# The last product of a decoder layer: twelve pairs of tiles in seven products, with their weight sums made by GpSimd and kept in DRAM

## The chip, the cores and the metric

One program on 1 core of a Trainium2 chip. The metric is device microseconds for one execution; the kernel before took 1563.09 us, the median of three runs (1562.99, 1563.09, 1564.04). Lower is better.

## The reference

One layer of a decoder on 256 tokens of width 2048, in float32. Three token mixers (a convolution A, a spatial gate B, a sparse attention C) are merged channel by channel by sigmoid gates, then a gated feed-forward of width 5632 follows. Cut to what matters here:

```python
h = rms_norm(x, w_pre);  p = h @ w_in                 # A, B, C inputs and 3 x 2048 gate logits
y = (g_A * A + g_B * B + g_C * C) @ w_o;  x = x + rms_norm(y, w_post)
h = rms_norm(x, w_pre2); u = causal_dwconv3(h @ w_up)
x = x + rms_norm((silu(u_g) * u_v) @ w_down, w_post2) # w_down: 5632 x 2048, "the last product"
```

## The kernel before

**Products.** Every float32 product is made as three TensorE products of rounded numbers: a weight tile arrives by a DMA of SyncE's queue in a buffer `wraw` (five of 128x1024, 512 KB each), ScalarE copies it, rounded, to `whi` (four), VectorE writes the remainder `wraw - whi` to `wlo` (four), and TensorE multiplies hi by hi, hi by lo and lo by hi. A load can be issued only when its buffer's last reader is done.

**Stages.** They follow each other on TensorE: the input projections (to about 296 us); the gating projections, function `branch`, with products `pg` and `py` (296 to 757); the product with `w_o` (757 to 842); the up projection (860 to 1325.7); the last product (1325.7 to 1553.4). In `branch` the work of the three mixers is cut in steps by Python generators, and `pump(BUDGET)` puts steps between the gating products. One of these steps is the compression of the attention's keys and values: `cmp_prep` copies pieces of `kd` into tiles `bt` (VectorE), whose last column GpSimd zeroes (`G.memset(tmp[:, :, :, 15], 0.0)`, L613), and splits them into `bk`, which TensorE takes in `zp`.

**What sets the order.** Up to the gating a scheduler with priorities orders the instructions of each engine. The splits of the weights follow a fixed order from `w_o` on, and in the last product everything does: `fixed` chains each instruction of ScalarE and VectorE behind the one before it, and `in_line` does so for TensorE. GpSimd has 48 instructions: some loads at the start, the copies to `kd`, the memsets of `bt`, the loads of `x2`, and `kept_y` and `yb`, by which the feed-forward's residual goes to DRAM and comes back.

**The last product.** The 44 tiles of 128 rows of `w_down` are taken in two halves of 1024 output columns (`Pair(0)`, `Pair(1)`). A plain tile costs 4 blocks x 3 = 12 matmuls of 128x512. Two tiles together are also done as a Strassen-like 2x2 product (Winograd's form): seven products instead of eight, 21 matmuls instead of 24. For that `quad` loads two pieces `b` and `a` (four blocks of 128x512) and forms four sums of them on VectorE, between the splits:

```python
fixed(V, V.tensor_sub, tt[:, L], b[:, L], a[:, U])
fixed(V, V.tensor_sub, a[:, U], a[:, U], a[:, L])
fixed(V, V.tensor_sub, tt[:, U], b[:, L], a[:, U])
fixed(V, V.tensor_sub, b[:, U], b[:, U], tt[:, U])
```

The sums of the activations of a pair are made by `sums` during the up projection. `EARLY` names ten such pairs, `PLAIN` the other 24 tiles; the last six of these are kept (`KEEP`), split in advance, and used block by block at the end of the second half: first tokens 0 to 127 with output columns `n` = 0 and 1, then tokens 128 to 255. Behind each block VectorE adds the side products (`result`), ScalarE squares, and after each token half come the norm (L247 to L250), the weighing by the gain, the scalings with the residual `yb` (L1418) and the writes. Tile `fin`, in the place that `hT` had, holds the results, the gain and two scratch pieces for the sums.

Of the kernel before, what the change touches and what calls it, by code (L numbers as in the profile page):

```python
# [31 lines left out]
T = 256  # L32
# [22 lines left out]
def block(ctx: ExitStack, tc: tile.TileContext, x, xf, fp, cst, rows, sgw, w1, w2, wf_a, wt_bv, wf_bu, wf_c,  # L55
# [289 lines left out]
    rh = PZ.tile([128, 2], F32, name="rh")  # L347
# [530 lines left out]
    BUDGET = BG  # L878
    mac = s16(P0, [128, 2, D], F32, "mac")
    mix = {}  # L880

    def branch(bi, act_of):

        for cb in range(4):
            pg = [PS.tile([128, 512], F32, tag="acc", name=f"pg{bi}{cb}{t}") for t in range(2)]
            for q in range(4):
                hs = granule(wt_g[(bi * 4 + cb) * 4 + q])
                for k in range(4 * q, 4 * q + 4):
                    hi, lo = hs[(k % 4) // 2]
# [15 lines left out]
            for q in range(2):  # L905
                hs = granule(wt_p[(bi * 4 + cb) * 2 + q])
                if cb == 0 and q == 0:
                    until("BAC"[bi])
                    if bi == 2:
                        mix["h"] = s16(P1, [128, KT, T], R, "mh")  # L910
                        mix["l"] = s16(P1, [128, KT, T], R, "ml")
                act = act_of()
                for k in range(4 * q, 4 * q + 4):
                    hi, lo = hs[(k % 4) // 2]
                    c = slice((k % 2) * 512, (k % 2) * 512 + 512)
                    for t in range(2):
# [105 lines left out]
    for cb in range(3):  # L1022
# [21 lines left out]
    for n, (cb, p) in enumerate(HELD):  # L1044
        for i in range(2):
# [184 lines left out]

    P2c = ctx.enter_context(tc.tile_pool(name="p2c", bufs=1))
    fin = P0.tile([128, 7168], F32, tag="hT", name="fin")
    res = fin[:, 0:4096].rearrange("p (t n) -> p t n", t=2)
    gain = fin[:, 4096:5120]
    turn = [0]

    def scratch():
        turn[0] ^= 1  # L1240
# [9 lines left out]
    def high(hi, x):  # L1250
        fixed(S, S.activation, hi, x, AF.Copy)

    def rest(lo, x, hi):
        fixed(V, V.tensor_sub, lo, x, hi.bitcast(F32))

    def weights(src, into=None):
        raw = fetch(src, 1024)
        hi, lo = (into[:, 0], into[:, 1]) if into is not None else ring(raw.name)
        high(hi, raw)
        rest(lo, raw, hi)  # L1260
        return hi, lo

    def ring(name):
        return P0.tile([128, 1024], R, tag="whi", bufs=4, name=f"whi{name}"), rests(f"wlo{name}")[:, 0:1024]

    class Pair:
        def __init__(self, p):
# [25 lines left out]

        def quad(self, j):

            k0, k1 = EARLY[j]
            last = j == len(EARLY) - 1
            b, a = (fetch(wt_dq[self.p, j][:, x:x + 1024], 1024) for x in (0, 1024))
            L, U = slice(0, 512), slice(512, 1024)
            nm = f"q{self.p}_{j}"  # L1300
            tt = scratch()
            (hb, lb), (ha, la), (ht, lt) = (ring(nm + x) for x in "bat")
            h4, l4 = (P2c.tile([128, 512], R, tag=tag, name=f"{tag}{nm}") for tag in ("h4", "l4"))
            high(hb, b)
# [12 lines left out]
            s1, s2, s4 = ((sh[:, i], sl[:, i]) for i in range(3))
            for bank_, act, (h, l), c in (
                    (self.c[0][1], s4, (hb, lb), L), (self.c[0][0], g2(k1, H1), (hb, lb), U),
                    (self.p1, g2(k0, H1), (ha, la), L), (self.p5, s1, (ha, la), U),  # L1320
                    (self.p7, g2(k0, H2), (ht, lt), L), (self.p6, s2, (ht, lt), U),
                    (self.c[1][0], g2(k1, H2), (h4, l4), L)):
# [37 lines left out]
    first, second = Pair(0), None  # L1360
    i = 0
    for j in range(NQ):
        while i < 3 + (NP - 6) * j // (NQ - 1):
            first.plain(i)
            i += 1
        first.quad(j)
    for i in range(i, NP):
        first.plain(i)
    first.combine()
    second = Pair(1)  # L1370
    kept = []
    i = 0
    for j in range(NQ):
        while i < 3 + (NP - KEEP - 3) * j // (NQ - 1):
            second.plain(i)
            if i == 2:
                for t in range(2):
                    for n in range(2):
                        first.result(t, n, fixed)
            elif 3 <= i < 7:  # L1380
                first.weigh((i - 3) // 2, (i - 3) % 2, fixed)
            elif i == 9:
                nc.sync.dma_start(gain, row(3072, 1024))
            i += 1
        second.quad(j)
        if j == len(EARLY) - 1:
# [3 lines left out]
        for x in range(0 if j < NQ - 5 else 1 if j < NQ - 1 else KEEP - 4):  # L1390
            k = NP - KEEP + len(kept)
            into = None
            if j < NQ - 1:
                kt = P2.tile([128, 11, T], R, tag=("gh", "gl")[j % 2], bufs=4, name=f"kept{k}")
                into = kt[:, 0:8].rearrange("p (a b) c -> p a (b c)", a=2)
            kept.append((PLAIN[k], weights(wt_dn[1, k], into)))
    assert i == NP - KEEP and len(kept) == KEEP
    second.combine()
    for t in range(2):
        for n in range(2):  # L1400
            c = slice(n * 512, n * 512 + 512)
# [20 lines left out]
def _layout(inp):  # L1422
# [110 lines left out]
```

## Time and profile before

| | |
|---|---|
| median of the runs | 1563.09 us |
| the profiled execution's own time | 1564.15 us |
| its span | 1562.4 us |
| TensorE busy (PE) | 1551.2 us, 99% |
| VectorE busy (DVE) | 1244.8 us, 80% |
| ScalarE busy (ACT) | 889.3 us, 57% |
| GpSimd busy (POOL) | 19.2 us, 1%, 50 instructions |
| DMA | 307.96 MB, mean 197 GB/s |
| granted TensorE clock | 0.998 |

The busy times are of one profiled execution; its own time stands 1.75 us over the span and 1.06 us over the median of the runs. A share of the span is an average over the stages. In the rows of the profile "L1282" is line 1282 of the kernel; a row of groups gives the line, engine, operation, output and inputs with their shapes, the count, the busy us and mean ns, and last the idle time of the engine ahead of these instructions with what ended most of it. A row of the timeline starts with its time from the span's start and its length, and ends in square brackets with the idle time before it, where there is any, and what released it.

### The profile page before, as it was taken

The numbers are of one execution on the slowest core, as the hardware profiler recorded it, in microseconds if no ns is written. First come the engines' busy times: TensorE is split into PE (matmuls) and PEld (weight loads), VectorE is DVE, ScalarE is ACT, GpSimd is POOL, SyncE is SP. The second block draws the span as 40 slices with busy tenths as digits, with TensorE's granted clock in tenths as the row PEclk, the third lists the DMA queues.
The fourth block names the chain that finished last, engine by engine and source line by source line (L and its number), as shares of the span: only waits on it lengthen the run. The fifth ranks groups of instructions, "written<-read, shape, count | busy, mean of one in ns | idle before, by whom it ended". The sixth has DMA issues, their size and how long they took to land.

```text
span 1562.4 us, 22642 instructions
## 1 busy us (share of the span) xinstructions
PE 1551.2 (99%) x8178; PEld 1316.5 (84%) x8178; DVE 1244.8 (80%) x2370; ACT 889.3 (57%) x1442; POOL 19.2 (1%) x50
## 2 busy tenths in 40 slices
PE   9999999999999999999999999999999999999997
PEld 7888889888888787788888888888888888888885
DVE  7899999857866555465567998888888888888997
ACT  7654454447646675644455665565555555555663
POOL 1000020000000000000000000000000000000000
PEclk9999999999999999999999999999999999999999
DMA  9565556666764445466774666666666666666674
GB/s 377 182 197 185 193 177 215 197 192 180 234 201 161 151 147 169 156 189 188 243 245 144 215 193 196 195 190 196 191 190 197 194 193 195 200 208 202 215 236 156
DMA packets 85441, 307.96 MB, mean 197 GB/s; under 512 B 9808, under 2 KB 10832, under 8 KB 84304
## 3 DMA queue, kind: packets, MB, share of 16 engines
q1 hardware_dynamic: 83376, 297.84, 60.0%
q0 software_dynamic: 1520, 8.39, 1.5%
q8 instruction: 64, 1.05, 0.3%
q14 instruction: 49, 0.40, 0.1%
q10 hardware_dynamic: 432, 0.28, 0.1%
HBM read 301.23 MB, written 4.19 MB: 195 GB/s over the span
## 4 chain that ended last, share of the span: by engine, by line
PE 96%; DVE 2%; DMA 1%; issue 0%; ACT 0%; DVEq 0%; POOL 0%; ACTq 0%; POOLq 0%
PE ps L190 29%; PE ps L197 15%; PE pg L211 6%; PE pg L210 6%; PE pg L212 6%; PE pd0b L1282 5%; PE pd1a L1282 4%; PE py L211 3%; PE py L212 3%; PE py L210 3%; PE po L210 2%; PE po L211 2%; PE po L212 2%; PE pd0a L1282 2%; PE pd1b L1282 1%; PE pv L210 1%
## 5 line engine op out<-in xcount | busy, mean ns | idle before, releaser
L149 ACT ACTIVATE whi<-wraw 128x1024 fp32r<-128x1024 f32 x440 | 461.9, 1054 | 250.8 <-PE pg L212 95.8
L151 DVE TENSOR_TENSOR wlo<-wraw,whi 128x1024 fp32r<-128x1024 f32 (+1 forms) x187 | 226.4, 1216 | 156.5 <-ACT whi L149 155.8
L163 DVE TENSOR_TENSOR wlo<-wraw,whi 128x896 fp32r<-128x896 f32 (+1 forms) x506 | 325.8, 685 | 12.1 <-ACT whi L149 7.3
L190 PE MATMUL ps<-h2T,whi 128*128 128x512 f32 x1360 | 323.1, 389 | 0.0
L190 PEld LDWEIGHTS ps<-h2T,whi 128*128 128x128 f32 x1360 | 249.2, 188 | 46.8
L197 PEld LDWEIGHTS ps<-h2T,wlo 128*128 128x128 f32 x1360 | 167.0, 188 | 6.7
L197 PE MATMUL ps<-h2T,wlo 128*128 128x256 f32 x1360 | 168.9, 277 | 0.0
L190 PE MATMUL ps<-hT,whi 128*128 128x512 f32 x640 | 156.6, 391 | 0.0
L212 PE MATMUL pg<-whi,hT 128*128 128x512 f32 x384 | 150.9, 393 | 0.0
L211 PE MATMUL pg<-wlo,hT 128*128 128x512 f32 x384 | 150.7, 392 | 0.0
L232 ACT ACTIVATE t<-ps 128x256 f32<-128x256 f32 x125 | 47.4, 380 | 175.9 <-PE ps L190 175.9
L210 PE MATMUL pg<-whi,hT 128*128 128x512 f32 x384 | 147.3, 393 | 0.0
L190 PEld LDWEIGHTS ps<-hT,whi 128*128 128x128 f32 x640 | 115.8, 188 | 21.1
L493 DVE SCALAR_TENSOR_TENSOR cv<-hb,fps,cv 128x256 f32<-128x256 f32 x240 | 104.2, 475 | 0.0
L233 DVE TENSOR_TENSOR t<-ps,t 128x256 f32<-128x256 f32 x125 | 52.6, 421 | 50.4 <-ACT t L232 50.4
L197 PEld LDWEIGHTS ps<-hT,wlo 128*128 128x128 f32 x640 | 82.0, 188 | 4.5
L211 PEld LDWEIGHTS pg<-wlo,hT 128*128 128x128 f32 x384 | 72.1, 188 | 16.2 <-issue 1.1
L212 PEld LDWEIGHTS pg<-whi,hT 128*128 128x128 f32 x384 | 72.1, 188 | 15.1 <-issue 0.7
L197 PE MATMUL ps<-hT,wlo 128*128 128x256 f32 x640 | 84.3, 278 | 0.0
L210 PEld LDWEIGHTS pg<-whi,hT 128*128 128x128 f32 x384 | 71.8, 188 | 14.8 <-issue 0.3
L998 DVE TENSOR_TENSOR wlowraw<-wraw,whiwraw 128x1024 fp32r<-128x1024 f32 x44 | 53.2, 1222 | 11.6 <-ACT whiwraw L998 10.2
L998 ACT ACTIVATE whiwraw<-wraw 128x1024 fp32r<-128x1024 f32 x44 | 45.7, 1055 | 18.0 <-PE pd0b L1282 15.0
(1021 smaller groups left out, 2517.3 us busy)
## 6 DMA issues: line engine op xcount, KB each, us to landing
wraw<-in_wf_up_dram SPq DMA_DIRECT2D x176, 512.0 KB, 4.4
wraw<-in_wt_g_dram SPq DMA_DIRECT2D x96, 512.0 KB, 4.3
wraw<-in_wt_p_dram SPq DMA_DIRECT2D x48, 512.0 KB, 3.8
wraw<-in_wt_dn_dram SPq DMA_DIRECT2D x48, 512.0 KB, 4.2
wraw<-in_wt_dq_dram SPq DMA_DIRECT2D x40, 512.0 KB, 4.5
wraw<-in_wf_a_dram SPq DMA_DIRECT2D x32, 512.0 KB, 4.2
wraw<-in_wt_o_dram SPq DMA_DIRECT2D x32, 512.0 KB, 4.6
wraw<-in_wf_bu_dram SPq DMA_DIRECT2D x16, 512.0 KB, 3.9
```

The costliest lines, as they stand in the source:

```text
L149: S.activation(hi[:, :n], raw[:, :n], AF.Copy)
L151: V.tensor_sub(lo[:, :n], raw[:, :n], hi[:, :n].bitcast(F32))
L163: V.tensor_sub(*x)
L190: ins = PE.matmul(ps[:, :, ts], lhsT=ws[k // 8][0][:, c:c + 128], rhs=mov[:, k, :, ts], start=(k == 0 and not t), stop=(k == n - 1), skip_ ...
L197: ins = PE.matmul(ps[:, 1, ts], lhsT=ws[k // 8][1][:, c:c + 128], rhs=mov[:, k, 0, ts], start=False, stop=False, skip_group_check=True).ins
L210: PE.matmul(ps, lhsT=xh, rhs=hi, start=first, stop=False)
L211: PE.matmul(ps, lhsT=xh, rhs=lo, start=False, stop=False)
L212: return PE.matmul(ps, lhsT=xl, rhs=hi, start=False, stop=last).ins
L233: V.tensor_add(t1 if rb is not None else dst, ps[:, 0], t1)
L493: V.scalar_tensor_tensor(ca[:, j], hb[:, j, k:k + T], w(j, k), ca[:, j], op0=ALU.mult, op1=ALU.add)
L998: seq[eng] = [op(*args, **kw).ins]
L1282: ins = PE.matmul(bank, lhsT=a[x], rhs=w[y], start=first and j == 0, stop=last and j == 2).ins
```

## The change

- Two more pairs, `LATE`, tiles (22, 23) and (24, 25), are done in seven products: 12 pairs, 20 plain tiles, four of them kept. The last product has 984 matmuls of 128x512, not 996. The activation sums of the two new pairs are made during the first half (`late`, step "L").
- The order of the steps in each half is spelled out by strings: P plain, Y a pair, L `late`, R result, W weigh, G gain, B `yb`, K keep.
- The weight sums of all 24 groups (2 halves x 12 pairs) are made by GpSimd in `weight_sums`, which `branch` advances by one step after each of its 72 stretches of products. A group has three steps: two loads of 512 KB by GpSimd's queue into one buffer `wsum`; two subtractions with a write each (256 KB, 512 KB); two more subtractions and a write of 512 KB, all to the DRAM tile `made`. The last product then loads `b` from the weights and the rest from `made`, three and a half pieces a group instead of two, and VectorE makes no sums there.
- Buffers: in the last product the loads go round six buffers (`wraw` x5 and a spare one), the rounded copies round five; `hT`, `h2k` and `h2T` move to a pool of their own that is closed before the last product.

```diff
+LATE = [(22, 23), (24, 25)]
+PLAIN = [*range(26, 33), 10, 21, *range(33, NFT)]
+PAIRS = EARLY + LATE
+FIRST = "PPYPPPYLYPPYLYPPPPYPYYPPPYYPYPYPPP"
+SECOND = "PPPRRRRYWPWYPYWPYWGYPYPYPYKPPKYPPYPPPBYYKK"
+MADE = [(p, j) for p, steps in enumerate((FIRST, SECOND)) for j, c in enumerate(c for c in steps if c in "QY") if c == "Y"]
...
+    def weight_sums():
+        for n, (p, j) in enumerate(MADE):
+            y = P1.tile([128, 2560], F32, tag="wsum", name=f"wsum{n}")
+            L, U = slice(0, 512), slice(512, 1024)
+            b, a, t = y[:, 0:1024], y[:, 1024:2048], y[:, 2048:2560]
...
+            G.dma_start(b, wt_dq[p, j][:, 0:1024])
+            G.dma_start(a, wt_dq[p, j][:, 1024:])
+            yield
+            G.tensor_sub(t, b[:, L], a[:, U])
+            G.dma_start(made[n, :, 1024:1536], t)
+            G.tensor_sub(a[:, U], a[:, U], a[:, L])
+            G.dma_start(made[n, :, 0:1024], a)
+            yield
+            G.tensor_sub(b[:, L], b[:, L], a[:, U])
+            G.tensor_sub(b[:, U], b[:, U], b[:, L])
+            G.dma_start(made[n, :, 1536:], b)
+            yield
+    making, now = weight_sums(), [None]
...
                         mm_t(pg[t], hT[:, k, 0, ts], hT[:, k, 1, ts], hi[:, c], lo[:, c], k == 0, k == KT - 1)
+                now[0] = hs[1][1]
+                if bi >= 0:
+                    next(making, None)
...
     branch(2, lambda: Ct_box["t"])
+    for _ in making:
+        pass
...
         def quad(self, j):
+            if (self.p, j) in MADE:
+                m = made[MADE.index((self.p, j))]
+                b, a, t = (weights(x) for x in (wt_dq[self.p, j][:, 0:1024], m[:, 0:1024], m[:, 1024:2048]))
+                return self.seven(j, b, a, t, split(load(m[:, 2048:], 512)[:, 0:512], (fourth("h4"), fourth("l4"))))
...
-    NP, NQ, KEEP = len(PLAIN), len(EARLY), 6
...
+    def late(j):
+        k0, k1 = LATE[j]
+        tmp = scratch(f"sums{j}", F32)
+        a = tmp[:, 0:512].rearrange("p (k t) -> p k t", k=2)
+        gi, gk = divmod(k0, 11)
+        fixed(V, V.tensor_add, a, gh[gi][:, gk:gk + 2].bitcast(F32), gl[gi][:, gk:gk + 2].bitcast(F32))
+        sums(tmp[:, 512:].rearrange("p (s t) -> p s t", s=4), a[:, 0], a[:, 1], k0, sums_at(len(EARLY) + j), fixed)
```

GpSimd's queue in the gating projections, at the memsets of `bt`. In a row stand the line, the operation, output and inputs with the shape, and the semaphores waited for. Before, the copies to `kd` and then the memsets:

```order
L602 DMA kd<-kcv 64x256 [waits DMASW6_49]
L603 DMA kd<-kcv 64x255 [waits DMASW7_49]
L613 MEMSET bt_3996 128x16 [waits DVE_49,PE_49]
L613 MEMSET bt_4004 128x16 [waits DVE_49,Pool_49]
L613 MEMSET bt_4050 128x16 [waits DVE_49,PE_49]
L613 MEMSET bt_4058 128x16 [waits DVE_49]
L613 MEMSET bt_4260 128x16 [waits DVE_49]
```

Now (L899 and L900 are the loads of a group, L902 to L908 its subtractions, L903, L905 and L909 its writes, L620 the memsets of `bt`):

```order
L899 DMA wsum_4037<-in_wt_dq_dram 128x1024 [waits DMASW7_49,DMASW6_49,DMASW0_49]
L900 DMA wsum_4037<-in_wt_dq_dram 128x1024
L620 MEMSET bt_4057 128x16 [waits DVE_49,PE_49]
L620 MEMSET bt_4065 128x16 [waits DVE_49]
L620 MEMSET bt_4115 128x16 [waits DVE_49,PE_49]
L620 MEMSET bt_4123 128x16 [waits DVE_49]
L902 TENSOR_TENSOR wsum_4037<-wsum_4037 128x512 [waits DMASW2_49,DMASW1_49]
L903 DMA made<-wsum_4037 128x512 [waits Pool_49]
L904 TENSOR_TENSOR wsum_4037<-wsum_4037 128x512
L905 DMA made<-wsum_4037 128x1024 [waits Pool_49]
L907 TENSOR_TENSOR wsum_4037<-wsum_4037 128x512
L908 TENSOR_TENSOR wsum_4037<-wsum_4037 128x512 [waits Pool_49]
```

The first four memsets now stand behind the loads of the sixth group (its first load waits for the fifth group's writes), and the second four behind that group's subtractions.

VectorE in the last product, one pair of tiles. Before, four sums between three remainders of 128x1024 and one of 128x512:

```order
L998 TENSOR_TENSOR fin<-wraw_13262,wraw_13264 128x512
L998 TENSOR_TENSOR wraw_13264<-wraw_13264 128x512
L998 TENSOR_TENSOR wloq_1b<-wraw_13262,whiq_1b 128x1024
L998 TENSOR_TENSOR fin<-wraw_13262,wraw_13264 128x512
L998 TENSOR_TENSOR wloq_1a<-wraw_13264,whiq_1a 128x1024
L998 TENSOR_TENSOR wraw_13262<-wraw_13262,fin 128x512
L998 TENSOR_TENSOR wloq_1t<-fin,whiq_1t 128x1024
L998 TENSOR_TENSOR l4q_1_13273<-wraw_13262,h4q_1_13272 128x512
```

Now (L1038 is what L998 was; `u`, `h` and `l` are the loaded piece, its rounded copy and its remainder), with the plain tile ahead of the pair:

```order
L1038 TENSOR_TENSOR l_13499<-u_13496,h_13498 128x1024
L1038 TENSOR_TENSOR l_13517<-u_13514,h_13516 128x1024
L1038 TENSOR_TENSOR l_13523<-u_13520,h_13522 128x1024
L1038 TENSOR_TENSOR l_13529<-u_13526,h_13528 128x1024
L1038 TENSOR_TENSOR l_13_13535<-u_13532,h_13_13534 128x512
```

The four sums are gone from the queue, and the remainders stay.

VectorE at the end of the first token half, where L1188 (now L1228) are the additions and weighings of `result` and `weigh`, `pd1a` the blocks of the product, L247 to L250 (now L254 to L257) the norm's steps, L1418 (now L1506) the scalings. Before:

```order
L1188 TENSOR_TENSOR fin<-pd1a_14015,fin 128x512
L315 TENSOR_REDUCE ssvd_14891<-ss_13116 128x1
L316 TENSOR_SCALAR ssvd_14891<-ssvd_14891 128x1
L1188 TENSOR_TENSOR fin<-fin 128x512
L247 RECIPROCAL rsyd_14894<-rsyd_14894 128x1
L248 TENSOR_TENSOR rstd_14895<-rsyd_14894 128x1
L249 SCALAR_TENSOR_TENSOR rstd_14895<-rstd_14895,ssvd_14891 128x1
L250 SCALAR_TENSOR_TENSOR rsyd_14894<-rstd_14895,rsyd_14894 128x1
L1418 SCALAR_TENSOR_TENSOR fin<-fin,rsyd_14894,yb 128x512 x4
L1188 TENSOR_TENSOR fin<-pd1a_14016,fin 128x512
L1188 TENSOR_TENSOR fin<-fin 128x512
L1348 TENSOR_TENSOR fin<-pd1a_14017,fin 128x256
```

Now:

```order
L1228 TENSOR_TENSOR res<-pd1a_14305,res 128x512
L321 TENSOR_REDUCE ssvd_15214<-ss_13368 128x1
L322 TENSOR_SCALAR ssvd_15214<-ssvd_15214 128x1
L1228 TENSOR_TENSOR res<-res,gain 128x512
L254 RECIPROCAL rsyd_15217<-rsyd_15217 128x1
L255 TENSOR_TENSOR rstd_15218<-rsyd_15217 128x1
L1228 TENSOR_TENSOR res<-pd1a_14306,res 128x512
L256 SCALAR_TENSOR_TENSOR rstd_15218<-rstd_15218,ssvd_15214 128x1
L257 SCALAR_TENSOR_TENSOR rsyd_15217<-rstd_15218,rsyd_15217 128x1
L1506 SCALAR_TENSOR_TENSOR res<-res,rsyd_15217,yb 128x512 x4
L1228 TENSOR_TENSOR res<-res,gain 128x512
L1423 TENSOR_TENSOR res<-pd1a_14307,res 128x256
```

The third block's addition (of `pd1a_14306`) has moved from behind the four scalings to a place inside the norm's steps.

More of the change, by code (lines that the diff above doesn't have):

```diff
@@ L1254, in rest, with cycle, take, spare @@
         fixed(V, V.tensor_sub, lo, x, hi.bitcast(F32))
-    def weights(src, into=None):
[L1257 to L1264, printed above, removed]
+    def cycle(makers):
+        n = [0]
+        def take(name, *args):
+            n[0] += 1
+            return makers[(n[0] - 1) % len(makers)](name, *args)
+        return take
+    def spare(x):
+        return lambda name, dt=R: P2d.tile([128, 1024], dt, tag=f"y{x}", name=name)
+    def extra(x):
+        return lambda name, dt=R: P2c.tile([128, 1024], dt, tag=f"x{x}", name=name)
+    def tagged(tag, bufs, dtype):
+        return [lambda name, dt=dtype: P0.tile([128, 1024], dt, tag=tag, bufs=bufs, name=name)] * bufs
+    raws_of = cycle(tagged("wraw", 5, F32) + [spare(1)])
+    whi = cycle(tagged("whi", 4, R) + [spare(0)])
+    wlo = cycle([lambda name, dt=R: rests(name)[:, 0:1024]] * 4)
+    scratch = raws_of
+    count = [0]
+    def load(src, n=1024):
+        count[0] += 1
+        to = raws_of(f"u{count[0]}", F32)
+        nc.sync.dma_start(to[:, :n], src)
+        return to
+    def split(x, into=None):
+        hi, lo = into or (whi(f"h{count[0]}"), wlo(f"l{count[0]}"))
+        high(hi, x)
+        rest(lo, x, hi)
+        return hi, lo
+    def weights(src, into=None):
+        return split(load(src), into)
+    def fourth(tag):
+        return P2c.tile([128, 512], R, tag=tag, name=f"{tag}_{count[0]}")
     class Pair:
@@ L1355, in weigh, with keep @@
             do(V, V.tensor_mul, self.at(t, n), self.at(t, n), gain[:, n * 512:n * 512 + 512])
-    NP, NQ, KEEP = len(PLAIN), len(EARLY), 6
[L1360 to L1363, printed above, removed]
+    def late(j):
[5 more added lines that the diff above has]
+        sums(tmp[:, 512:].rearrange("p (s t) -> p s t", s=4), a[:, 0], a[:, 1], k0, sums_at(len(EARLY) + j), fixed)
+    def keep():
+        n = len(kept)
+        into = None
+        if n < SECOND.count("K") - 2:
+            kt = P2.tile([128, 11, T], R, tag=("gh", "gl")[n % 2], bufs=4, name=f"kept{n}")
+            into = [kt[:, 4 * x:4 * x + 4].rearrange("p b c -> p (b c)") for x in range(2)]
+        k = SECOND.count("P") + n
+        kept.append((PLAIN[k], weights(wt_dn[1, k], into)))
+    first, kept = Pair(0), []
+    i = j = n = 0
+    for c in FIRST:
+        if c == "P":
             first.plain(i)
             i += 1
-        first.quad(j)
-    for i in range(i, NP):
-        first.plain(i)
+        elif c == "L":
+            late(n)
+            n += 1
+        else:
+            first.quad(j)
+            j += 1
     first.combine()
     second = Pair(1)
[L1371 to L1374, printed above, removed]
+    i = j = n = 0
+    for c in SECOND:
+        if c == "P":
             second.plain(i)
[L1376 to L1383, printed above, removed]
-            i += 1
-        second.quad(j)
-        if j == len(EARLY) - 1:
+            i += 1
+        elif c == "R":
+            first.result(n // 2, n % 2, fixed)
+            n += 1
+        elif c == "W":
+            first.weigh((n - 4) // 2, n % 2, fixed)
+            n += 1
+        elif c == "G":
+            nc.sync.dma_start(gain, row(3072, 1024))
+        elif c == "B":
             yb = s16(P0, [128, 2, D], F32, "yb")
@@ L1389, in block @@
                 G.dma_start(yb[:, t], kept_y[:, t])
[L1390 to L1397, printed above, removed]
+        elif c == "K":
+            keep()
+        else:
+            second.quad(j)
+            j += 1
     second.combine()
+    P2d.tile([128, 120], F32, name="fill2")
     for t in range(2):
```

78 lines of the change are left out of this document (43 added, 35 removed).

## The prediction

> **What bounds the kernel now.** I read the page first: TensorE's busy share and the chain that ended last.
>
> ```profile
> PE 1551.2 (99%) x8178; PEld 1316.5 (84%) x8178; DVE 1244.8 (80%) x2370; ACT 889.3 (57%) x1442; POOL 19.2 (1%) x50
> ...
> PE 96%; DVE 2%; DMA 1%; issue 0%; ACT 0%; DVEq 0%; POOL 0%; ACTq 0%; POOLq 0%
> ```
>
> TensorE is the bound nearly everywhere: 96% of the chain is its own work, so only fewer products, or a stall of it, can move the time. Next come the table by stage (columns: stretch, its length, then busy us and instruction count of PE, PEld, DVE, ACT, POOL, then granted clock, DMA share, GB/s) and the chain in order of time, for the last product.
>
> ```profile
> 34.70:36.30 1.60, 1.60 (x9) 1.33 (x8) 1.55 (x3) 1.55 (x5) 1.60 (x4) 1.00 1.03 422
> ...
> 296.00:757.00 461.00, 461.00 (x2233) 373.84 (x2232) 287.25 (x555) 266.30 (x492) 2.66 (x11) 1.00 0.58 181
> ...
> 1325.00:1438.00 113.00, 113.00 (x500) 93.55 (x499) 100.46 (x116) 65.11 (x69) 0.00 (x0) 1.00 0.65 207
> 1438.00:1536.00 98.00, 97.28 (x425) 79.12 (x424) 92.90 (x109) 60.25 (x69) 0.00 (x0) 1.00 0.65 209
> ```
>
> ```profile
> 1325.74 9.52 PE pd0b L1282 x42
> ...
> 1438.62 9.52 PE pd1a L1282 x42
> ...
> 1512.35 4.45 DMA wraw<-in_wt_dq_dram
> 1523.55 5.22 DMA wraw<-in_wt_dq_dram
> 1536.40 17.04 PE pd1a L1282 x75
> ```
>
> One matmul of 512 columns takes 9.52/42 = 0.2267 us. A half of the last product has 24 plain tiles of 12 matmuls and 10 groups of 21, so 498: 112.9 us. The first half takes exactly that (1325.74 to 1438.62). The second ends at 1536.40 + 17.04 = 1553.44, so it takes 114.8; 0.2 of the excess is the last matmul's own length, and about 1.8 is stall, around the two late loads. VectorE is 95% busy there (92.90 of 98).
>
> **The change, part by part.** *Products.* Two more pairs turn 48 matmuls per half into 42. Twelve fewer in all: 12 x 0.2267 = 2.7 us, on the path, since TensorE is the path.
>
> *The stall.* VectorE's work for a group, by its rows:
>
> ```profile
> L998 DVE TENSOR_TENSOR wlowraw<-wraw,whiwraw 128x1024 fp32r<-128x1024 f32 x44 | 53.2, 1222 | 11.6 <-ACT whiwraw L998 10.2
> ...
> L998 DVE TENSOR_TENSOR fin<-wraw,wraw 128x512 f32<-128x512 f32 x40 | 27.4, 685 | 3.1 <-DMA wraw<-in_wt_dq_dram 3.0
> ...
> L998 DVE TENSOR_TENSOR l4q<-wraw,h4q 128x512 fp32r<-128x512 f32 x20 | 13.7, 684 | 0.7 <-ACT h4q L998 0.7
> ```
>
> Before: three rests of 1.22, one of 0.68, four sums of 0.685: 7.1 us, against 21 x 0.2267 = 4.8 of TensorE, so consecutive groups run late and free their load buffers late. After: 4.3 us, under TensorE's 4.8. The 1.8 us should go. What replaces it is DMA: a group reads 512 KB x 3.5 = 1.84 MB, not 1.05, so a half reads 20 x 0.524 + 12 x 1.84 = 32.5 MB in 111.5 us, 292 GB/s; the first row of that table shows 422, so 512 KB can take 1.24 us. Three and a half pieces take 4.3 us in a group's 4.8: it fits, with six load buffers, not five. The two late pairs' sums (six VectorE operations of at most 0.69 us) lie in the first half, where VectorE now has slack. I cost them at nothing.
>
> *The tail.* Six tiles kept to the end become four, so each of the four output blocks has 12 matmuls behind it, 2.72 us, not 4.08. VectorE around the last three blocks:
>
> ```profile
> 1545.30 0.69 DVE L1188 TENSOR_TENSOR fin<-pd1a,fin 128x512 f32<-128x512 f32 x1 [1.91 <-PE pd1a L1282]
> ...
> 1547.84 0.16 DVE L248 TENSOR_TENSOR rstd<-rsyd 128x1 f32<-128x1 f32 x1
> ...
> 1548.42 2.74 DVE L1418 SCALAR_TENSOR_TENSOR fin<-fin,rsyd,yb 128x512 f32<-128x512 f32 x4
> 1551.07 0.69 DVE L1188 TENSOR_TENSOR fin<-pd1a,fin 128x512 f32<-128x512 f32 x1
> 1552.61 0.69 DVE L1188 TENSOR_TENSOR fin<-fin 128x512 f32<-128x512 f32 x1 [0.85 <-ACT junk L1188]
> 1553.46 0.42 DVE L1348 TENSOR_TENSOR fin<-pd1a,fin 128x256 f32<-128x256 f32 x1 [0.15 <-PE pd1a L1282]
> ```
>
> From the first token half's last add (1545.30) to its norm's second step takes 2.54, to the end of the four scalings about 5.8. Now the third block's add comes 2.72 after the first row and is queued behind that second step; it waits for TensorE until 2.72, takes 0.6, then two small steps (0.4), the scalings (2.65 from start to next start) and a weighing (0.65): the last add starts 7.05 after the first row. TensorE is done 5.44 after it, so VectorE is 1.6 us late where it was on time (1553.46). Minus 1.6 of the gain.
>
> *The sums made early.* GpSimd gets 120 DMA issues and 96 subtractions of 128x512, between the first gating product and the start of w_o. Where TensorE has its margin there:
>
> ```profile
> L149 ACT ACTIVATE whi<-wraw 128x1024 fp32r<-128x1024 f32 x440 | 461.9, 1054 | 250.8 <-PE pg L212 95.8
> ```
>
> ScalarE's splits wait for TensorE to free buffers, so pieces normally lie ready, and the 56.6 MB (24 x 2.36) raise 181 GB/s over 461 us to 304, still below 422. I take that as hidden except at one place, the first compression of the attention. POOL's, VectorE's and TensorE's rows there:
>
> ```profile
> 386.56 0.13 POOL L613 MEMSET bt<- 128x16 f32 x1 [161.37 <-DVE At L535]
> ...
> 389.36 0.12 POOL L613 MEMSET bt<- 128x16 f32 x1
> 397.07 0.13 POOL L613 MEMSET bt<- 128x16 f32 x1 [7.59 <-DVE bk L621]
> ```
>
> ```profile
> 386.00:412.00 26.00, 26.00 (x131) 22.04 (x131) 23.12 (x55) 18.84 (x32) 1.02 (x8) 1.00 0.69 216
> ```
>
> ```profile
> 391.85 1.01 DVE L616 TENSOR_SCALAR bt<-kd,fps 128x60 f32<-128x60 f32 x5
> ...
> 396.60 0.75 DVE L621 TENSOR_TENSOR bk<-bt,bk 128x256 fp32r<-128x256 f32 x2
> ...
> 399.08 1.22 DVE L151 TENSOR_TENSOR wlo<-wraw,whi 128x1024 fp32r<-128x1024 f32 x1
> ```
>
> ```profile
> 398.06 0.28 PE L632 MATMUL zp<-whi,bk 128*128 128x256 f32 x1
> ...
> 400.42 0.43 PE L211 MATMUL pg<-wlo,hT 128*128 128x512 f32 x1
> ```
>
> VectorE is 89% busy; TensorE takes bk 0.71 us after it is made (396.60 + 0.75) and a rest 0.12 after it (399.08 + 1.22). Any delay of VectorE from 390 to 402 passes to TensorE. Whether GpSimd delays it, these rows tell:
>
> ```profile
> 22.18 0.91 POOL L358 TENSOR_SCALAR fps<-fps 128x248 f32<-128x248 f32 x1 [20.24 <-DMA fps<-in_fp_dram]
> ...
> 22.32 0.88 DVE L121 TENSOR_TENSOR rwraw<-wraw,swraw 128x512 fp32r<-128x512 f32 x1
> ```
>
> ```profile
> 29.31 0.69 DVE L121 TENSOR_TENSOR rwraw<-wraw,swraw 128x512 fp32r<-128x512 f32 x1 [0.16 <-ACT swraw L120]
> ```
>
> ```profile
> L366 POOL TENSOR_SCALAR_AFFINE_SELECT rsg<-rsg x8: 286/472/742, 33.6 to 36.8; 128x128 f32<-128x128 f32 x8
> ```
>
> Beside a GpSimd pass over 248 elements a two-input subtraction of VectorE takes 0.88 us, not 0.69: 0.19 lost. Scaled to 512 elements and two operands: 0.8 us per GpSimd subtraction that meets one; nothing, if they don't meet; at most the whole GpSimd operation, 4 x 0.286 = 1.14 (an estimate from the fastest 128-element row). The fifth group's chain (counting from zero) should fill the gap from 389.4 to 397.1 (four subtractions and three issues: 4 x 1.14 + 3 x 0.54 = 6.2), the sixth's come after about 404. About a third of VectorE's time there is one-input work, so 4 x 0.8 x 2/3 = 2.1, less the margin, plus a remainder of the sixth: I take 2.0, between 0 and 8 x 1.14 = 9.1, nearest to the row that shows 0.19. The Trainium skill (SBUF — State Buffer, section on SBUF's two separate sides) calls the shared port pair an exclusive lock, held for the full instruction by a VectorE operation with two SBUF inputs or a GpSimd one. By that rule the VectorE row at 22.32 should have lost much of GpSimd's 0.91; the trace shows 0.19, so the measurement decides the size, and the rule only that there is a loss. With the rule the sum would come out as the third rival's.
>
> A pair of 512 KB loads bunched in front of the gating loads there costs 0 to 2.5 us (2 x 1.24); I take 0.5, since the margins elsewhere take it.
>
> *The sum:* -2.7 - 1.8 + 1.6 + 2.0 + 0.5 = -0.4 us on the profiled execution of 1564.15 (span 1562.4, 1.75 around it). The median of the runs, 1563.09, is 1.06 under it; 1563.1 - 0.4 = 1562.7.
>
> **The rivals.** *Hidden after all.* GpSimd meets VectorE where it has slack: -2.9, 1560.2; with the tail's 1.6 overestimated, 1558.6. For it: VectorE is busy 287 of 461 us. Against it: the 89% above.
>
> *GpSimd comes late to its memsets.* It runs in order; the four memsets of bt now stand behind the loads of group five, and VectorE's adds need them at 391.85, with everything of VectorE queued behind those adds. A group takes, from these rows
>
> ```profile
> wraw<-in_wt_g_dram SPq DMA_DIRECT2D x96, 512.0 KB, 4.3
> ...
> kept_y<-y POOLq DMA_DIRECT2D x2, 1024.0 KB, 4.5
> ```
>
> ```profile
> 830.97 0.54 POOL L1166 DMA_DIRECT2D kept_y<-y  x1 [77.44 <-DVE y L988]
> ```
>
> ```profile
> L210 PE MATMUL pg<-whi,hT x384: 387/389/585, 296.5 to 740.4; 128*128 128x512 f32 x192
> ```
>
> loads 4.8 (0.54 + 4.3), subtractions 4.6, two issues 1.1, the last write 4.2: 14.7 us. From 296.5, five of them and two issues end at 371: in time. It decides from 18.8 us a group; a subtraction of 0.91 x 512/248 = 1.9 and landings a microsecond longer give 20, the memsets at 397.6, and 5.8 - 0.7 = 5.1 of stall: -2.9 + 5.1 + 1.5 for what then meets later = +3.7, about 1566.8. This is the case on the other side.
>
> *The port is held throughout.* Eight subtractions at 1.14, two thirds of them met: 6 us, with the 0.5: -2.9 + 6.5 = +3.6, 1566.7.
>
> **How the numbers follow.** About 0.2% (3.1 us) is what a measurement of this kernel can tell from no change. The forecast (within 3.1 of before): 0.55. Hidden: 0.24, of which I put 0.19 below 1560.0 and the rest just inside. Late memsets: 0.13. Port held: 0.08. So faster 0.19, same 0.60, slower 0.21. The range is 1558.9 to 1567.5: its low end is the first rival without most of the tail's loss, its high end takes in both costly rivals. The forecast's own range is 1560 to 1566.
>
> **What would show it.** The last product's 984 matmuls in 223 us without a wait for DMA; its start (1325.74) moved by the gating's cost, about +2.5; VectorE's last 128x256 adds beginning some 1.6 us after TensorE is done; POOL's memsets of bt before 391.9; a TensorE wait between 390 and 412 and nowhere else before w_o. I am wrong if TensorE waits all over the gating, if GpSimd still makes sums when x2's load is due (752), or if last-product pieces land late at 292 GB/s.

## The result: 1.24% slower, all of it lost ahead of the up projection

The changed kernel takes 1582.62 us (median of six runs, 1576.19 to 1591.74), against 1563.56 for before in the same comparison: ratio 1.0124, 95% interval 1.0109 to 1.0139. The range given was 1558.9 to 1567.5. Its runs spread over 15.5 us, those of before over 1.5. Every rival of the prediction was too small. The page of the changed kernel, at the places of the page before:

```profile
PE 1555.1 (98%) x8166; PEld 1318.4 (83%) x8166; DVE 1273.7 (80%) x2312; ACT 895.6 (57%) x1454; POOL 234.4 (15%) x268
...
PE 80%; issue 6%; DMA 5%; DVE 4%; POOL 3%; ACT 2%; DVEq 0%; POOLq 0%; ACTq 0%
```

TensorE's share of the chain fell from 96% to 80%: DMA, VectorE and GpSimd now set the end of stretches. TensorE's own timeline tells in which stage. First the first matmul of the last product before, then after, then the last one before and after:

```profile
1325.58 0.39 PE L1282 MATMUL pd0b<-whiwraw,gh 128*128 128x512 f32 x1
```

```profile
1348.84 0.39 PE L1349 MATMUL pd0b<-h,gh 128*128 128x512 f32 x1
```

```profile
1553.03 0.39 PE L1282 MATMUL pd1a<-whiwraw,gl 128*128 128x512 f32 x1
```

```profile
1571.78 0.39 PE L1349 MATMUL pd1a<-h,gl 128*128 128x512 f32 x1
```

The last product starts 23.3 us late (1348.84 - 1325.58) and is 4.5 us shorter (222.9 against 227.5). VectorE's last scaling starts 7.30 us behind TensorE's last matmul, where it was 5.79: 1.5 more. So 23.3 - 4.5 + 1.5 = 20.3; the profiled executions differ by 1584.46 - 1564.15 = 20.3. The last product did what was forecast. The stretch from the start of the gating to the start of the up projection cost 23 us in place of 2.5.

TensorE's waits from the start of the gating to that of the up projection (columns: total us, times, longest); before, there was no wait of this kind in that stretch:

```profile
PE zp L639 <- DVE bk L628: 6.4, 1, 6.4
PE pg L218 <- DVE wlo L158: 3.8, 3, 2.5
PE po L217 <- ACT whi L156: 2.5, 1, 2.5
PE pp L831 <- DVE am L802: 1.3, 1, 1.3
PE po L218 <- DVE wlo L158: 0.9, 1, 0.9
PE zp L641 <- DVE wlo L158: 0.6, 1, 0.6
```

They make 15.5 us. Another part is clock. Three stretches behind a wait, in the columns of the prediction's table by stage (the granted clock is third from the end):

```profile
384.90:388.90 4.00, 3.93 (x11) 3.07 (x12) 4.00 (x9) 3.62 (x7) 1.08 (x2) 0.59 0.95 269
...
409.00:413.00 4.00, 3.80 (x14) 3.31 (x15) 3.51 (x7) 4.00 (x7) 0.00 (x0) 0.51 0.88 281
...
827.70:833.60 5.90, 4.95 (x14) 3.70 (x15) 5.11 (x6) 3.88 (x4) 0.00 (x0) 0.71 0.81 263
```

Behind waits of 2.5, 6.4 and 2.5 us the granted clock is 0.59, 0.51 and 0.71 over these 4.0, 4.0 and 5.9 us, which costs 0.41 x 4.0 = 1.6, then 2.0 and 1.7 us: 5.3 in all. The other 2.5 of the 23.3 us lie at the same places and show neither as a listed wait nor as clock. Behind the wait of 1.3 us at 545 the clock stayed at 1.00. The Trainium skill (TensorE: Matmul & The Clock Gate, Part 1) says that the clock goes back to half after an idle window of about 3.4 us; the half rate agrees with these rows, but here gaps of 2.5 us were enough, and in e2 (below) one of 2.05 us, at 816.7, was.

Comparing the start of the same matmul in both traces gives the lateness place by place (0.1 us that the trace after already has at 296 is taken off):

| place in the trace after | lateness there, us | what TensorE waited for |
|---|---|---|
| 382 to 389 | 0 to 4.4 | VectorE's remainder, late |
| 402 to 413 | 4.4 to 13.0 | `bk` of the first compression |
| 416 to 424 | 13.0 to 15.8 | VectorE's remainders |
| 545 | 16.0 to 17.5 | VectorE's `am` of the attention |
| 824 to 834 | 17.5 to 23.1 | weights of `w_o` |

**Why VectorE is late.** Eight multiplications of 128x256 with both inputs in SBUF stand at the same place of VectorE's timeline before and after:

```profile
374.77 2.77 DVE L529 TENSOR_TENSOR cv<-cv,rsya 128x256 f32<-128x256 f32 x8
```

```profile
375.76 8.01 DVE L536 TENSOR_TENSOR cv<-cv,rsya 128x256 f32<-128x256 f32 x8
```

GpSimd's timeline around it: the load and the four subtractions of the fourth group, the first subtraction of the fifth, and the first memsets of `bt` (in brackets the idle time before and what ended it):

```profile
366.14 0.55 POOL L899 DMA_DIRECT2D wsum<-in_wt_dq_dram  x1 [4.77 <-DMA made<-wsum]
...
375.86 1.48 POOL L902 TENSOR_TENSOR wsum<-wsum 128x512 f32<-128x512 f32 x1 [8.64 <-DMA wsum<-in_wt_dq_dram]
...
378.24 1.30 POOL L904 TENSOR_TENSOR wsum<-wsum 128x512 f32<-128x512 f32 x1
...
380.43 1.31 POOL L907 TENSOR_TENSOR wsum<-wsum 128x512 f32<-128x512 f32 x1
381.82 1.34 POOL L908 TENSOR_TENSOR wsum<-wsum 128x512 f32<-128x512 f32 x1
...
395.27 2.35 POOL L902 TENSOR_TENSOR wsum<-wsum 128x512 f32<-128x512 f32 x1 [6.91 <-DMA wsum<-in_wt_dq_dram]
...
408.02 0.28 POOL L620 MEMSET bt<- 128x16 f32 x4
```

GpSimd's four subtractions take 1.48 + 1.30 + 1.31 + 1.34 = 5.43 us, and VectorE's run is 8.01 - 2.77 = 5.24 longer: it stands still nearly for GpSimd's whole time. The other way round it is the same: the fifth group's first subtraction starts 0.03 us behind a remainder of VectorE and takes 2.35 us, not 1.3, while the remainder keeps its time.

```profile
395.24 1.23 DVE L158 TENSOR_TENSOR wlo<-wraw,whi 128x1024 fp32r<-128x1024 f32 x1 [1.08 <-ACT whi L156]
```

That is the rule of the Trainium skill (SBUF — State Buffer, section on who interferes with whom), an exclusive lock for the whole instruction, which the prediction set aside for one row with 0.19.

**Why the memsets are late:** from 296 a group starts every 22 us or so, and the four memsets stand behind the loads of the sixth, at 408. ScalarE's copies of `bt` wait for them:

```profile
ACT bk L627 <- POOL bt L620: 10.9, 1, 10.9
```

**Why `w_o` waits:** 24 groups end at 813, not by 752, so that GpSimd's last transfers and subtractions, and x2's loads behind them, meet the loads and splits of `w_o`. GpSimd's timeline, then the chain in order of time:

```profile
813.23 1.08 POOL L994 DMA_DIRECT2D x<-in_x_dram  x2
```

```profile
808.91 5.51 DMA wraw<-in_wt_o_dram
...
816.79 8.78 DMA wraw<-in_wt_o_dram
```

### The profile page after: what moved, and what is told of

Its sections match the earlier page's. It is cut to its first block, busy times and chain, and to the rows that moved or that the text cites. A ratio compares the mean times of both kernels' runs of the same rounds, so it can differ in the third digit from the quotient of the medians.

```text
span 1582.8 us, 23113 instructions
## 1 busy us (share of the span) xinstructions
PE 1555.1 (98%) x8166; PEld 1318.4 (83%) x8166; DVE 1273.7 (80%) x2312; ACT 895.6 (57%) x1454; POOL 234.4 (15%) x268
## 4 chain that ended last, share of the span: by engine, by line
PE 80%; issue 6%; DMA 5%; DVE 4%; POOL 3%; ACT 2%; DVEq 0%; POOLq 0%; ACTq 0%
PE ps L197 26%; PE ps L204 13%; PE pd0b L1349 5%; PE pd1a L1349 5%; PE pg L218 4%; PE pg L219 4%; PE pg L217 4%; DMA wsum<-in_wt_dq_dram 3%; PE pd1b L1349 2%; PE pd0a L1349 2%; PE py L218 2%; PE py L219 2%; PE py L217 2%; PE po L218 1%; PE po L219 1%
## 5 line engine op out<-in xcount | busy, mean ns | idle before, releaser
L158 DVE TENSOR_TENSOR wlo<-wraw,whi 128x1024 fp32r<-128x1024 f32 (+1 forms) x187 | 261.3, 1406 | 117.6 <-ACT whi L156 116.3
L1038 DVE TENSOR_TENSOR l<-u,h 128x1024 fp32r<-128x1024 f32 (+1 forms) x134 | 147.9, 1128 | 48.5 <-ACT h L1038 27.6
L1038 ACT ACTIVATE h<-u 128x1024 fp32r<-128x1024 f32 (+1 forms) x134 | 127.1, 980 | 68.2 <-PE pd1a L1349 25.6
L500 DVE SCALAR_TENSOR_TENSOR cv<-hb,fps,cv 128x256 f32<-128x256 f32 x240 | 108.4, 502 | 0.0
```

Of the source, the lines that this page charges most:

```text
L158: V.tensor_sub(lo[:, :n], raw[:, :n], hi[:, :n].bitcast(F32))
L500: V.scalar_tensor_tensor(ca[:, j], hb[:, j, k:k + T], w(j, k), ca[:, j], op0=ALU.mult, op1=ALU.add)
L1038: seq[eng] = [op(*args, **kw).ins]
```

## The experiments

Time is the median; "start" is that of the last product's first matmul (before: 1325.6, after: 1348.8), "length" from there to its last (227.5, 222.9). The kernel before was timed anew beside each run; its medians were 1563.5 to 1564.0. In e3 to e6 and e14 some or all of the sums are left out, so these five do not compute the layer; they separate causes.

| run | time, us | ratio to before, interval | start | length |
|---|---|---|---|---|
| e1: all sums by VectorE | 1579.2 | 1.0094 (1.0080 to 1.0108) | 1325.5 | 241.3 |
| e2: memsets on VectorE | 1583.5 | 1.0112 (1.0096 to 1.0128) | 1347.9 | 223.0 |
| e3: no subtractions | 1568.8 | 1.0035 (1.0024 to 1.0046) | 1332.7 | 223.0 |
| e4: subtractions only | 1568.4 | 1.0028 (1.0017 to 1.0039) | 1332.3 | 223.3 |
| e5: no subtractions, memsets on VectorE | 1561.4 | 0.9986 (0.9977 to 0.9995) | 1325.4 | 222.9 |
| e6: 19 groups | 1577.5 | 1.0088 (1.0075 to 1.0102) | 1343.9 | 222.9 |
| e14: 19 groups, memsets on VectorE | 1573.8 | 1.0065 (1.0051 to 1.0079) | 1337.1 | 223.0 |
| e7: 12 groups by GpSimd, begun late, six kept | 1569.0 | 1.0037 (1.0023 to 1.0051) | 1325.3 | 232.6 |
| e8: as e7, four kept | 1565.5 | 1.0013 (1.0004 to 1.0022) | 1325.3 | 226.7 |
| e9: 14 groups, begun late, five kept | 1566.7 | 1.0024 (1.0013 to 1.0035) | 1325.8 | 228.0 |
| e10: 16 groups, two early, five kept | 1562.1 | 0.9995 (0.9987 to 1.0004) | 1325.8 | 224.1 |
| e11: 16 groups, four kept | 1563.1 | 0.9998 (0.9989 to 1.0007) | 1325.8 | 224.5 |
| e12: 16 groups, moved | 1568.4 | 1.0028 (1.0018 to 1.0037) | 1325.8 | 231.0 |
| e13: 17 groups, three early | 1561.5 | 0.9989 (0.9980 to 0.9998) | 1327.0 | 223.0 |

**e1.**

```diff
-FIRST = "PPYPPPYLYPPYLYPPPPYPYYPPPYYPYPYPPP"
+FIRST = "PPYPPPYLYPPYLYPPPPYPYYPPPYYPYPYPPP".replace("Y", "Q")   # Q: VectorE makes the sums; SECOND likewise
```

> All twelve pairs, but no sums made by GpSimd in the gating stage: the last product forms them on VectorE as before (same strings, buffers and tail as the changed kernel). If the whole loss arises in the gating stage, its 23.1 us go: the last product starts at 1325.7 again, saves 2.7 by twelve fewer matmuls, loses 1.6 in the tail, and keeps the stall of 1.8 or more, since VectorE has 7.1 us for a pair: about 1562.5 to 1566, on the level of before. If some of the loss lies in the last product itself (buffers, order), it stays above 1570.

The gating is free of waits and the start is that of before, so the whole 23 us belongs to GpSimd's work. The time missed its range by 13 us, though: the last product takes 241.3 us, because it is VectorE that makes the sums here. Its two halves in the table by stage:

```profile
1325.70:1440.00 114.30, 110.43 (x474) 87.92 (x473) 107.19 (x137) 66.31 (x77) 0.00 (x0) 1.00 0.61 196
1440.00:1567.00 127.00, 121.25 (x512) 94.06 (x510) 115.33 (x144) 69.88 (x86) 1.08 (x2) 1.00 0.54 188
```

VectorE is busy for 107 of 114 and 115 of 127 us there, and TensorE waits for it (8 us in all): in this order of the steps, twelve pairs do not go with VectorE's sums. Against that, the sums from DRAM are worth 241.3 - 222.9 = 18.4 us. The prediction's 1.8 is another difference, the stall of before with its ten pairs.

**e2.**

```diff
-            G.memset(tmp[:, :, :, 15], 0.0)
+            V.memset(tmp[:, :, :, 15], 0.0)
```

> The changed kernel with the eight memsets of bt on VectorE, so that GpSimd's groups cannot make them late. The theory that GpSimd's order is to blame (memsets at 408 behind five groups of 22 us): the wait of 6.4 us at 402 goes with its half-clock time, 8 to 11 us in all, 1572 to 1575; the waits at 382 and 824 stay. The theory that the memsets are only where a delay of VectorE shows: under 3 us, 1580 or more.

```profile
PE pg L218 <- DVE wlo L158: 4.7, 3, 3.3
PE po L218 <- DVE wlo L158: 3.7, 3, 2.0
PE zp L639 <- DVE bk L628: 3.2, 1, 3.2
PE po L217 <- ACT whi L156: 1.6, 1, 1.6
```

The time is the second theory's (1580 or more), but not for its reason. The wait for `bk` halved (6.4 to 3.2) and did not go, since VectorE, held, is late at `bk` by itself. By the comparison of matmuls TensorE leaves the gating 12.5 us late, not 17.5, so the memsets cost 5.0 there; then the product with `w_o` loses 9.9, not 5.6 (the listed waits are 5.3 against 3.4), and takes nearly all of it back. Why it lost more there is not shown. e6 and e14 price the memsets without the waits at `w_o`.

**e3, e4 and e5** take GpSimd's work apart.

```diff
 e3:
-            G.tensor_sub(t, b[:, L], a[:, U])
-            G.dma_start(made[n, :, 1024:1536], t)
-            G.tensor_sub(a[:, U], a[:, U], a[:, L])
+            G.dma_start(made[n, :, 1024:1536], b[:, L])
...
-            G.tensor_sub(b[:, L], b[:, L], a[:, U])
-            G.tensor_sub(b[:, U], b[:, U], b[:, L])
 e4, in place of a group's loads and writes:
+            G.tensor_copy(b[:, 0:1], now[0][:, 0:1].bitcast(F32))
 e5: e3, and
-            G.memset(tmp[:, :, :, 15], 0.0)
+            V.memset(tmp[:, :, :, 15], 0.0)
```

> The changed kernel without the 96 subtractions (so the pieces in DRAM are not the sums); the loads and writes of GpSimd's queue stay, 57 MB. A group then takes about 22.4 - 6.5 = 16 us. If the subtractions hold VectorE's port and stretch the groups, all waits go: 1563.5 - 2.9 = 1560.7, up to 1563. If the transfers delay the gating loads, the waits stay: 1575 or more.

> The changed kernel with the 96 subtractions, four per three stretches of gating products, on constant data, and without GpSimd's loads and writes; the last product reads as many bytes, from the weights. GpSimd is then never late. If the port is held, VectorE's tensor_tensor takes 1.3 us longer per meeting and the waits at 382 and 545 stay (4.4 and 1.8, some more): 1565 to 1570. If only GpSimd's lateness costs, nothing is left: 1560 to 1562.

> The run without the subtractions, with the memsets of bt on VectorE besides: what is left in the gating stage are the 57 MB of GpSimd's transfers alone. If late memsets were all that cost the run without subtractions its 7 us (start of the last product), it starts at 1325.7 again and takes 1564.0 - 2.7 - 1.8 + 1.6 = 1561.1 (1560.5 to 1562). If the transfers themselves delay the gating loads, it stays at 1565 to 1569.

Transfers without subtractions (e3) start the last product 7.1 us late, by one wait:

```profile
PE zp L639 <- DVE bk L628: 4.7, 1, 4.7
```

and GpSimd's row says why: in this build the memsets stand behind the loads of the seventh group.

```profile
402.26 0.29 POOL L620 MEMSET bt<- 128x16 f32 x4
```

With these on VectorE (e5) no wait of TensorE is left from 296 to its end, and the time is 1561.4, as expected. So 57 MB through GpSimd's queue cost the gating loads nothing, and e3's expectation failed by the memsets alone. The subtractions without any transfer (e4) cost 6.7 us although the memsets are in time (391 to 393). The time is the one expected with the port held, but no wait is at 382: GpSimd's subtractions stand at 382 to 389 here, not at 376 to 383. The longest wait, with 0.6 and 0.4 in the attention behind it:

```profile
PE zp L639 <- DVE bk L628: 2.2, 1, 2.2
```

**e6 and e14** keep GpSimd's groups where they are and make only 19.

```diff
-        for n, (p, j) in enumerate(MADE):
+        for n, (p, j) in enumerate(MADE[:19]):
 ... (e14: with e2's line)
```

> The changed kernel with 19 groups made, not 24; the last five groups load as many bytes from the weights (their pieces are not the sums). By 19 x 22.4 us GpSimd ends near 722, before x2's loads are due (752). If x2's late loads cause the waits in the product with w_o (824 to 840), 5.5 us go: 1576 to 1578, and the waits at 382 and 402 stay. If those waits come from VectorE's lateness, or from GpSimd's writes, nothing changes: 1581 to 1583.

> The run with 19 groups with the memsets of bt on VectorE too: neither memsets nor x2's loads are behind GpSimd's groups; its subtractions stand beside the first compression as in the change. What is left is VectorE's lateness: waits of 2.5 to 3.3 at 382 and of about 3 at 402, each followed by some 2 us at half clock, and 2 to 3 near 420 to 430: the last product starts 11 to 12 us late, 1563.6 - 2.9 + 11.5 = 1572 (1570 to 1574). If late memsets were most of it, 1565 to 1568.

With 19 groups x2's loads start at 771, as soon as their tile is free, and no wait at `w_o` is left. The two longest:

```profile
PE zp L639 <- DVE bk L628: 9.0, 1, 9.0
PE pg L218 <- DVE wlo L158: 3.3, 2, 2.5
```

The start moves by 5.0 (1348.8 to 1343.9). The memsets on VectorE besides take the wait for `bk` from 9.0 to 3.2 and the start by another 6.8, to 1337.1. What is left, 1337.1 - 1325.6 = 11.5, arises between 380 and 435 and is VectorE held beside the first compression, with its half-clock time; without the subtractions (e5) it is gone. So the shares in the profiled executions are 11.5 (port), 6.8 (memsets) and 5.0 (the last five groups and x2): 23.3. Single executions do not give them so finely: the medians of e5, e14, e6 and the change (1561.4, 1573.8, 1577.5, 1582.6) make 12.3, 3.7 and 5.1, and e2 gave 5.0 for the memsets. By each count the port's share is the largest. Whether x2's loads, GpSimd's last writes or its last subtractions slowed `w_o` was not separated.

**e7 to e13** look for a place for the subtractions. "Begun late" means that the making starts with the second mixer's gating, behind the compression; with "early" two or three groups are made ahead of it. The other groups' sums are VectorE's (Q).

```diff
 e7, e8, e9:
-                if bi >= 0:
+                if bi >= 1:
 e10 to e12 (two groups early; the copy of n = 2 holds GpSimd until the second mixer):
+                if bi >= 1 or not cb:
-            if n == 0:
+            if n in (0, 2):
 e13 (three early; the first of the two lines as here, the second as in e10):
+                if bi >= 1 or 6 * cb + q < 9:
+            if n in (0, 3):
 FIRST:
 e7, e8    "PPQPPPYLQPPYLQPPPPYPQYPPPQYPQPYPPP"
 e9 to e11 "PPYPPPYLYPPYLQPPPPYPQYPPPQYPQPYPPP"
 e12, e13  "PPYPPPYLYPPYLYPPPPYPQYPPPQYPQPYPPP"
 SECOND:
 e7        "PPPRRRRQWPWYPQWPYWGQPYPQPYKPPKQPPYKPKBQYKK"
 e8        "PPPRRRRQWPWYPQWPYWGQPYPQPYKPPKQPPYPPPBQYKK"
 e9        "PPPRRRRQWPWYPQWPYWGQPYPQPYKPPKQPPYPPBQKYKK"
 e10, e13  "PPPRRRRQWPWYPYWPQWGYPYPQPYKPPKYPPQPPBYKYKK"
 e11       "PPPRRRRQWPWYPYWPQWGYPYPQPYKPPKYPPQPPPBYYKK"
 e12       "PPPRRRRQWPWYPQWPYWGQPYPYPQKPPKYPPQPPBYKYKK"
```

> Twelve pairs, every other group's sums made by GpSimd (12 of 24), the others by VectorE; the making starts with the second mixer's gating (about 450), behind all memsets of bt, and ends by 12 x 22.4 us near 720, before x2; six kept tiles as before. If order and port in the first compression make the loss, what is left is 1 to 3 us of waits near 530 to 550: 1564.0 - 2.7 - 1.8 + 2 = 1561.5 (1560 to 1563). If the port costs the same wherever GpSimd subtracts, half the groups cost half: 1570. If VectorE is late in the last product with six groups in a half, 1564 or more.

> The kernel with half of the groups made, but with four kept tiles at the end as in the change. If VectorE's last additions come 1.6 us late because the third block's addition and a weighing stand ahead of them, it takes 1.6 us longer than with six (1 to 2); if the tail is bound otherwise, the same within 0.3.

In e7 and e8 the gating costs nothing. In e8 TensorE is busy in all of the 258 us in which GpSimd makes its groups:

```profile
442.00:700.00 258.00, 258.00 (x1288) 204.20 (x1287) 166.89 (x329) 156.05 (x334) 103.23 (x107) 1.00 0.80 265
```

So e7's second case, a port that costs the same wherever GpSimd subtracts, is out, although its 1570 is near the 1569.0. Its third came true: the loss has moved to the last product (232.6 and 226.7, not 223), where VectorE is late again. e8 was to take 1 to 2 us longer than e7 and took 3.5 less: e7's two more kept tiles bring a wait of ScalarE for their place, so the two say nothing of the tail.

> Twelve pairs; 14 of the 24 groups made by GpSimd from the second mixer's gating on (14 x 21.6 us from 442: to about 745), among them the first five of the first half, where VectorE's own sums cost 3.1 us in the run with half of them; five kept tiles. If VectorE's lateness at the start of the last product and the tail's four kept tiles are what was left: 1563.6 - 2.7 - 1.8 + 0.5 = 1559.6 (1558.5 to 1561). If VectorE's sums cost wherever they stand: 1563 or more.

> As the run with 14, but two groups more, made in the first 40 us of the gating, ahead of the compression (GpSimd waits then until the second mixer's gating): 1559.0 (1558 to 1560.5) if GpSimd costs nothing away from the compression; 2 us more than the run with 14 if its subtractions cost there too.

> As the run with 16 made, but with four kept tiles, not five. If VectorE is 1.5 us late at the end with four: 1.0 to 1.6 us above that run; if not, within 0.3.

> As the run with 16 made and five kept tiles, but the made groups stand where VectorE is short: the first six groups of the first half are made (one pair's activation sums, made by VectorE, lie just ahead of the fifth), and seven of the second half. If the 1.6 us lost at 1364 come from a group of VectorE's own behind those sums, they go: 1562.1 - 1.5 = 1560.6 (1559.8 to 1561.5), 0.15 to 0.2% under before. If VectorE is then late at the next such group, 1562 as there.

> 17 groups made: three in the first 60 us of the gating, 14 from the second mixer's gating on; first half with the first six made (no wait at 1364), second half as in the run with 16 and five kept tiles (no wait there). If the waits belong to the places and not to the number of groups, neither the gating stage nor the last product waits: 1562.1 - 1.5 = 1560.6 (1559.8 to 1561.5). If the third early group or a longer making costs, 1562 or more.

e9, e10 and e12 missed their ranges. e10 (1562.1, not up to 1560.5) still loses about 1.2 us from 1364 on. e9 and e12 wait in the second half (length 228.0 and 231.0); e9 has a group of VectorE's own directly ahead of kept tiles near the end, e12 one more such group in that half than e10, but no run changes that alone, so this cause is argued and not shown. e10 and e11 differ by the kept tiles: VectorE's last scaling starts 6.24 us behind TensorE with five, 7.30 with four, and the times differ by 1.0. e13 joins e12's first half and e10's second and waits nowhere for more than 0.6 us:

```profile
PE pg L218 <- DVE wlo L158: 0.6, 1, 0.6
PE pp L831 <- DVE am L802: 0.2, 1, 0.2
```

At 0.9989 (0.9980 to 0.9998) it is, of the kernels that leave nothing out, the only one clearly under before, by 0.1%; its median is 21 us under that of the change.

## Why the prediction was wrong

**Right: the last product.** 12 matmuls less (2.7) and the stall gone (1.8) made 4.5, and 4.5 was measured. Neither half waits for a DMA at 281 to 298 GB/s, and VectorE has slack:

```profile
1348.80:1462.00 113.20, 113.20 (x500) 93.55 (x500) 87.10 (x97) 69.02 (x82) 0.00 (x0) 1.00 0.88 298
1460.60:1572.00 111.40, 111.40 (x493) 92.04 (x491) 83.96 (x90) 68.67 (x82) 1.08 (x2) 1.00 0.79 281
```

**Right: the tail.** The working gave 1.6; 1.5 was measured, and e11 against e10 shows 1.0 for a kept tile less. VectorE's queue, in the order that the prediction read, with the last addition 1.55 behind TensorE's end (1571.78 + 0.39):

```profile
1566.76 0.69 DVE L1228 TENSOR_TENSOR res<-pd1a,res 128x512 f32<-128x512 f32 x1 [0.55 <-PE pd1a L1349]
...
1569.48 0.69 DVE L1228 TENSOR_TENSOR res<-pd1a,res 128x512 f32<-128x512 f32 x1
...
1570.47 2.74 DVE L1506 SCALAR_TENSOR_TENSOR res<-res,rsyd,yb 128x512 f32<-128x512 f32 x4
...
1573.72 0.42 DVE L1423 TENSOR_TENSOR res<-pd1a,res 128x256 f32<-128x256 f32 x1
```

**Right: the transfers are hidden.** The 0.5 for bunched loads was even too much (e5: none).

**Wrong: the port's price.** The step "0.19 lost ... 0.8 us per GpSimd subtraction that meets one", 2.0 in the sum, is where it failed: 11.5 us was measured (12.3 by the medians), half clock included. Its row held two short operations, one of them on the engine whose spans are rough, and it was scaled by size; why that row shows only 0.19 is not known. Met by a subtraction, VectorE waits it out (5.24 of 5.43 us). The third rival had this mechanism, with 6 us and a chance of 0.08. Its upper bound of 1.14 per meeting was short: subtractions took 1.3 us, and 2.35 where VectorE had the port first. And the prediction looked for meetings from 390 to 402 only; the first wait was at 382, where its own rule (VectorE short of slack) held as well.

**Wrong: a group's length.** The step "14.7 us" made the memsets come in time; the rival named the point where that ends (18.8) and gave it 0.13. Measured over 24 groups: the subtractions 146 us (6.1 each, not 4.6), the waits for loads 163 (6.8) and for the last write 110 (4.6), five issues 68 (2.8), the rest hand-overs: about 21.5. The sum had three issues of the five, and the loads' and the write's latency came from rows of a kernel in which GpSimd's queue was nearly idle. The wrong reader was named, too: it was ScalarE's copies, not VectorE's additions, that waited for the memsets.

**Missing.** x2's lateness (5.0) stood among the things that would prove the prediction wrong, without a price, although 24 groups from 296.5 on need only 19.2 us each to pass 757. The half clock behind each wait had no term. And the rivals were priced one by one, where one cause, long groups with a held port, brings all of them at once.

## What to carry to other kernels

A second engine's "free" time is worth what it leaves the first one: GpSimd's subtractions were free where VectorE had slack (e7 and e8, from 442 on) and cost some 12 us in one stretch of 50 us where it had none. Work put into an in-order queue is priced by its whole round (loads, waits and writes under traffic), and then everything behind it in that queue, to the last, gets a due time. When a trace row and a rule of contention differ, look for more rows of that pair before one of them sets the price.

## What the runs showed of the hardware

Which of VectorE's operations GpSimd's subtractions hold shows in the groups of the gating stage, before (first fence) and after (second):

```profile
L795 DVE CUSTOM_DVE_ANT_0 ep<-s,cs 128x128 f32<-128x128 f32 (+1 forms) x64 | 18.7, 352 | 5.6 <-PE s L766 5.6
L929 DVE TENSOR_TENSOR mac<-mac,mg 128x256 f32<-128x256 f32 x32 | 12.4, 419 | 0.0
L926 DVE SCALAR_TENSOR_TENSOR mg<-mg,py 128x256 f32<-128x256 f32 x32 | 11.6, 415 | 4.0 <-ACT whi L149 2.7 <-PE py L212 1.2
L493 DVE SCALAR_TENSOR_TENSOR cv<-hb,fps,cv 128x256 f32<-128x256 f32 x13 | 5.7, 478 | 0.0
L616 DVE TENSOR_SCALAR bt<-kd,fps 128x60 f32<-128x60 f32 x32 | 6.3, 264 | 0.0
```

```profile
L802 DVE CUSTOM_DVE_ANT_0 ep<-s,cs 128x128 f32<-128x128 f32 (+1 forms) x64 | 18.7, 349 | 1.0 <-PE s L773 1.0
L967 DVE TENSOR_TENSOR mac<-mac,mg 128x256 f32<-128x256 f32 x32 | 17.1, 566 | 0.0
L964 DVE SCALAR_TENSOR_TENSOR mg<-mg,py 128x256 f32<-128x256 f32 x32 | 11.6, 414 | 1.2 <-ACT whi L156 1.2
L500 DVE SCALAR_TENSOR_TENSOR cv<-hb,fps,cv 128x256 f32<-128x256 f32 x13 | 7.8, 638 | 0.0
L623 DVE TENSOR_SCALAR bt<-kd,fps 128x60 f32<-128x60 f32 x32 | 11.3, 425 | 0.0
```

The operations that take one input from TensorE's output (`s`, `py`) kept their time, although 35 of the 64 with `s` ran beside a subtraction. Two inputs in SBUF went from 419 to 566 ns, and the one-input addition in `bt` from 264 to 425. The same kind of operation in the same size, SCALAR_TENSOR_TENSOR of 128x256, kept its 0.41 us with `py` and went from 478 to 638 ns with both tensors in SBUF (`hb`, `cv`). So for two inputs it is where they lie that decided here, and not the size or the kind. For one input in SBUF the kind does count: a TENSOR_REDUCE of 128x256 at 467.98 took its usual 0.42 us wholly beside a subtraction (467.56, 1.31 us), but that is one case.
